# Operand addresses modulo 256 bytes in a hybrid decoder layer: rows of x and of the convolution blocks, with k and v in 272 and 256 columns

## The chip, the cores and the metric

The kernel runs on one core of a Trainium2 chip. Its metric is the device time of one execution in microseconds (us); several executions give a median. One further execution was recorded by the hardware profiler, with the start and the length of every instruction and DMA; all rows below are of that one. The engines are TensorE (PE, with its weight loads as PEld), VectorE (DVE), ScalarE (ACT), GpSimd (POOL) and SyncE (SP), which issues DMAs here.

## What is computed

One layer over L = 528 tokens: 16 learned meta tokens ahead of 512 of x, width 2048. An RMS norm and one input projection give q, k, v (8 heads of 128) and b, c, u (1024 channels each):

```python
p = n @ w_in[l]
q, k, v, gb, gc, u = jnp.split(p, ...)
o_attn = _stick_breaking_attention(rmsnorm(q), rmsnorm(k), v)
o_conv = gb * _causal_dwconv(gc * u, conv_w[l])       # three taps: t-2, t-1, t
h = h + concat(rmsnorm(o_attn), rmsnorm(o_conv)) @ w_out[l]
h = h + (silu(n2 @ w_gate[l]) * (n2 @ w_up[l])) @ w_down[l]
return h[:, N_META:]
```

q and b are needed for the 512 tokens of x alone. k and v are needed for all 528, and c and u from two tokens before the first of x on.

## The kernel before, in words

Activations lie with channels on the 128 partitions and tokens along the free axis, in fp32. An fp32 product is made of three fp32r matmuls: each operand is split into a rounded part (hi) and the rest (lo), and weights hi x hi, hi x lo and lo x hi are summed in PSUM. So a k tile of 128 channels takes three matmuls per part of the columns (lines 280, 282 and 284 in `product_steps`; 742, 743 and 744 in `block_product`; 842 to 844 in `wide_product`). A bank of PSUM holds 512 columns.

**x.** `split_x` (line 347) makes for each of 16 k tiles two tiles nh and nl of 528 columns, 2112 B a partition, which lie one behind the other in the pool npool. They are the moving operands of all input projections.

**Attention** (to about 340 us). `head` (line 480) runs k, q and v of each of 8 heads as plain products over 16 k tiles. k and v take their 528 columns in two parts of H = 264, one in each bank; q takes 512 columns from column META = 16 on. `qk_norm`, and `attend` with its `sums` and `mix`, are queued with `after(n, ...)`, which runs them n k tiles later in the middle of the next products, so ACT and DVE work beside PE. `form_blocks` (line 414) runs eight times in this stage: it loads x again, split at column C0 = 8 into two halves of CH = 260 columns, forms four sums of quadrants on DVE, splits them into hi and lo, and stores them into the DRAM tensor fc (a run of 8 x 260 columns for each partition, block and part).

**Convolution columns, plain** (340 to 416 us). Two channel tiles j = 0, 1: c and u as plain products of two parts of CH = 260 columns from C0 (line 683), b with 512 (line 688). `conv_taps` multiplies c and u, and r2 (the squared token scale), and applies the three taps; `conv_out` multiplies by b and splits the result. After b of j = 0 the attention's pools are closed and six loads on POOL's queue bring three of the four blocks from fc into the tile blk (line 701). After b of j = 1 sixteen loads (line 708) overwrite the second halves of the first eight nh and nl with the fourth block.

**Convolution columns, block products** (416 to 598 us). The other six channel tiles go two at a time, three pair products for each two (c and u for each of two tiles, and b for both): `pair_product` (line 746) computes a 2 x 2 block product with seven instead of eight block multiplications of 24 matmuls, so 168 matmuls for a pair product. Of the seven moving blocks, three come from blk (of_blk) and four from nh and nl (parts_of). A pair product writes y, z and x in banks of its own, one after the other.

**The rest** (from 598 us): `wide_product` by w_out, 512 columns; then the gated network, 22 pair products over blocks of 256 columns held in `slots` (line 851), which puts 4 elements ahead of a block and 60 behind it; then w_down in the same way.

Order of the queues: all weight loads are on SP's queue (line 172, `load_at`), each issued when its buffer comes free; loads and stores of activations are on POOL's, except those of `load_x`, `form_blocks` and a few at the end, which are on SP's. DMAs of one queue are served in the order of their issue.

Of the kernel before, what the change touches and what calls it, by code (L numbers as in the profile page):

```python
# [33 lines left out]
def hybrid_layer(ctx: ExitStack, tc: tile.TileContext, xT, w_in, w_out, w_gu, w_down, vecs, out):  # L34
# [22 lines left out]
    pp = open_pool("pp", 2, space=PSUM)  # L57
    sm = open_pool("sm", 4, space=PSUM)

    n_tmp = [0]  # L60
# [260 lines left out]

    H = L // 2
    n_hl = []
    accs = [pool.tile([P, L], F32, name=f"acc_x{i}") for i, pool in enumerate((rpool, atmp))]
# [5 lines left out]
    def x_scale():  # L330
        ve.tensor_tensor(acc, acc, accs[1], ALU.add)
        for a in (0, H):
            ps = small(f"ssx{a}")
            pe.matmul(ps[:, :H], ones, acc[:, a : a + H], start=True, stop=True)
            ve.tensor_scalar(ms[:, a : a + H], ps[:, :H], 1.0 / D, EPS, ALU.mult, ALU.add)
# [11 lines left out]
    def split_x(k):  # L347
        nh = npool.tile([P, L], F32R, tag=f"nh{k}", name=f"nh{k}")
        nl = npool.tile([P, L], F32R, tag=f"nl{k}", name=f"nl{k}")
        g = g_mix[:, k : k + 1]  # L350
        sc.activation(nh, xts[k], AF.Copy, scale=g)
        ve.scalar_tensor_tensor(nl, xts[k], g, nh.bitcast(F32), ALU.mult, ALU.subtract)
        n_hl.append((nh, nl))

    def square_x(k):
        if k < 2:
            sc.activation(accs[k], xts[k], AF.Square)
        else:
            s = t512(L, "r", 3)
            sc.activation(s, xts[k], AF.Square)  # L360
            ve.tensor_tensor(accs[k % 2], accs[k % 2], s, ALU.add)

    pk0 = pp.tile([P, 2, 512], F32, tag="pp", name="pk0")
    pq0 = pp.tile([P, 2, 512], F32, tag="pp", name="pq0")
    steps = [
        product_steps([(pk0[:, 0, :H], 0, H), (pk0[:, 1, :H], H, L)], n_hl, KT),
        product_steps([(pq0[:, 0, :], META, L)], n_hl, KT),
# [42 lines left out]
    od = {}  # L410
    C0, CH = 8, (L - 8) // 2
    fc = dram.tile([P, 4, 2, 8, CH], F32R, name="fc")

    def form_blocks(k):
# [3 lines left out]
        for i, kk in ((0, k), (2, k + 8)):  # L418
            nc.sync.dma_start(x4[:, i : i + 2], two(xT[kk][:, C0:]))
        for i, kk in ((0, k), (2, k + 8)):  # L420
# [25 lines left out]
    def qk_norm(ps, g, cols, dst, parts_of, name):  # L446
# [8 lines left out]
        cuts = [(0, cols)] if cols == SEQ else [(0, H), (H, L)]  # L455
        raw_v, s_v = (raw, s) if cols == SEQ else (two(raw), two(s))
        sc.activation(s_v, ps, AF.Square)
        sc.activation(raw_v, ps, AF.Copy, scale=g)
        split(sh, sl, s)
# [20 lines left out]
    def head(h):  # L480

        if h:
            pk = pp.tile([P, 2, 512], F32, tag="pp", name=f"pk{h}")
            product([(pk[:, 0, :H], 0, H), (pk[:, 1, :H], H, L)], n_hl)
# [5 lines left out]
        after(8 if h else 11, qk_norm(halves(pk, H), g_k, L, kn[:, :L], (kh, kl, 384), f"k{h}"))  # L490
# [12 lines left out]
        product([(pv[:, 0, :H], 0, H), (pv[:, 1, :H], H, L)], n_hl)  # L503
        vt = t512(L, "e", 2)
        ve.tensor_tensor(two(vt[:, :L]), halves(pv, H), two(r), ALU.mult)
        after(6 if h else 11, lambda: attend(h, kn, kh, kl, qn, qh, ql, vt))
# [146 lines left out]
    def conv_taps(j, c1, c2, y):  # L653

        ve.tensor_tensor(c1, c1, two(r2[:, C0:]), ALU.mult)
        ve.tensor_tensor(c1, c2, c1, ALU.mult)
        cu = c1.rearrange("p a b -> p (a b)")
        o = META - 2 - C0
        sc.activation(y, cu[:, o : o + SEQ], AF.Copy, scale=cw[:, 3 * j : 3 * j + 1])
        for t in (1, 2):  # L660
            ve.scalar_tensor_tensor(
                y, cu[:, o + t : o + t + SEQ], cw[:, 3 * j + t : 3 * j + t + 1], y, ALU.mult, ALU.add
            )
# [12 lines left out]
    for j in range(CONV_FIRST):  # L676
# [4 lines left out]
        for c in (c1, c2):  # L681
            p = pp.tile([P, 2, 512], F32, tag="pp", name="pcu")
            product([(p[:, 0, :CH], C0, C0 + CH), (p[:, 1, :CH], C0 + CH, L)], n_hl)
            sc.copy(two(c), halves(p, CH))
# [6 lines left out]
        if j == 0:  # L691
# [14 lines left out]
    for k in range(8):  # L706
        for part in range(2):
            gp.dma_start(n_hl[k][part][:, C0 + CH :], fc[:, 1, part, k])

    def parts_of(kk, a):  # L710
        return lambda part, k: n_hl[kk + k][part][:, a : a + CH]

    def of_blk(i):
        return lambda part, k: blk[:, i, part, k]

    conv_acts = [
        parts_of(0, C0), of_blk(2), of_blk(0), of_blk(1), parts_of(0, C0 + CH), parts_of(8, C0), parts_of(8, C0 + CH)
    ]
# [67 lines left out]

    def pair(acts):
        c1, c2 = halves_of("e"), halves_of("e2")
        x = pair_product(acts, two(c1), two(c2), sides)
# [3 lines left out]
    for j in range(CONV_FIRST, HEADS, 2):  # L793
        ys = []
        for m in range(2):
            c1, c2 = pair(conv_acts)
# [16 lines left out]
        for m in range(2):  # L813
            s = t512(SEQ, "e", 2)[:, :SEQ] if j == HEADS - 2 else cpool.tile([P, SEQ], F32, tag="s", name=f"sq{j}_{m}")
            with tc.high_priority(1 << 20) if j == HEADS - 2 else ExitStack():
                conv_out(j + m, gbs[m][:, META - C0 :], ys[m], slots[m][:, 0], slots[m][:, 1], s, ve)
    oc = [oc_end[:, 2], oc_end[:, 3], *(oc_mid[:, i] for i in range(HEADS - 2 - CONV_FIRST)), oc_end[:, 0], oc_end[:, 1]]
# [40 lines left out]
    def slot(pool, dt, n, tag, name, **kw):  # L858
        return slots(pool, dt, 1, n, name, tag=tag, **kw)[0]

    def pad(pool, n):
        pool.tile([P, n // 4], F32, name=f"pad_{pool.name}")

# [370 lines left out]
```

## Time and profile before

| what | value |
|---|---|
| median of 3 runs | 2044.49 us (2041.42 to 2046.47) |
| the profiled execution's own time | 2048.55 us |
| its span, first to last instruction | 2046.8 us |
| PE, DVE, ACT, POOL busy | 2032.0, 1718.8, 1051.1, 381.2 us |
| mean granted clock of TensorE | 0.998 of full speed |

The profile's page gives busy times of each engine, the chain of work that ended last, and the costliest groups of instructions. A group's mean duration is from the start to the modelled end of one instruction; matmuls are pipelined, so a matmul's duration is longer than the time from its start to the next one's start. That time, the step, is read from the start times of the timeline.

### The profile page before, as it was taken

What the parts mean: (1) busy time and instruction counts of PE and PEld (TensorE: products, weight loads), DVE (VectorE), ACT (ScalarE), POOL (GpSimd) and SP (SyncE); (2) the same over time, 40 slices, a digit from 0 to 9 for tenths busy, and PEclk for the clock granted to TensorE, in tenths of its full rate; (3) what the DMA queues carried; (4) which work ended last, traced back from release to release, by engine and by line L of the source; (5) the groups of instructions that cost most, each with busy time, mean ns of one, the idle gap of its engine ahead of it and who ended that gap; (6) DMA issues with size and microseconds to landing.
All of it is one profiled execution on the core that took longest, in us unless ns stands there. A gap on an engine that the chain in (4) does not pass through costs nothing.

```text
span 2046.8 us, 39727 instructions
## 1 busy us (share of the span) xinstructions
PE 2032.0 (99%) x16158; PEld 1969.1 (96%) x16158; DVE 1718.8 (84%) x2202; ACT 1051.1 (51%) x1517; POOL 381.2 (19%) x533
## 2 busy tenths in 40 slices
PE   9999999999999999999999999999999999999999
PEld 8999999999998888999999999999999999999999
DVE  8788878588876777998998998998998998888887
ACT  7666666344443435545555545554554544444443
POOL 0111111210015441011111111111101252223111
PEclk9999999999999999999999999999999999999999
DMA  6333344743365556566565565555555999989864
GB/s 230 100 129 116 127 138 130 254 149 104 104 211 181 184 181 205 155 174 171 150 176 150 151 175 153 154 171 158 151 174 152 274 311 314 246 237 255 231 156 89
DMA packets 161591, 361.70 MB, mean 177 GB/s; under 512 B 13568, under 2 KB 73216, under 8 KB 161408
## 3 DMA queue, kind: packets, MB, share of 16 engines
q1 hardware_dynamic: 79200, 227.94, 34.8%
q0 software_dynamic: 82208, 131.23, 24.4%
q8 instruction: 127, 2.08, 0.4%
q14 instruction: 56, 0.46, 0.1%
HBM read 278.50 MB, written 80.61 MB: 175 GB/s over the span
## 4 chain that ended last, share of the span: by engine, by line
PE 92%; DVE 3%; ACT 2%; DMA 2%; issue 2%; POOL 1%; SPq 0%; DVEq 0%; ACTq 0%; POOLq 0%
PE x L742 13%; PE x L744 13%; PE x L743 13%; PE z L742 6%; PE z L743 6%; PE z L744 6%; PE y L743 3%; PE y L742 3%; PE y L744 3%; PE po L843 2%; PE po L842 2%; PE po L844 2%; PE pv L280 2%; PE pv L284 1%; PE pv L282 1%
## 5 line engine op out<-in xcount | busy, mean ns | idle before, releaser
L188 ACT CAST s_buf<-w_buf 128x1024 fp32r<-128x1024 f32 (+2 forms) x665 | 660.5, 993 | 772.6 <-PE x L743 348.7
L189 DVE TENSOR_TENSOR s_buf<-w_buf,s_buf 128x1024 fp32r<-128x1024 f32 (+2 forms) x665 | 767.8, 1155 | 173.9 <-ACT s_buf L188 173.4
L743 PE MATMUL x<-f,s_buf 128*128 128x256 f32 x1408 | 388.5, 276 | 4.2 <-DMA f<-fx 4.2
L742 PE MATMUL x<-f,s_buf 128*128 128x256 f32 x1408 | 388.5, 276 | 0.5 <-ACT sides L772 0.5
L744 PE MATMUL x<-f,s_buf 128*128 128x256 f32 x1408 | 388.4, 276 | 0.0
L201 DVE TENSOR_TENSOR w_buf<-w_buf 128x1024 f32<-128x1024 f32 (+1 forms) x243 | 277.6, 1142 | 14.2 <-DMA w_buf<-w_in 9.9
L743 PEld LDWEIGHTS x<-f,s_buf 128*128 128x128 f32 x1408 | 265.4, 188 | 4.4 <-DMA f<-fx 4.4
L742 PEld LDWEIGHTS x<-f,s_buf 128*128 128x128 f32 x1408 | 265.3, 188 | 1.2 <-ACT sides L772 0.9
L744 PEld LDWEIGHTS x<-f,s_buf 128*128 128x128 f32 x1408 | 265.4, 188 | 0.0
L1036 POOL DMA_DIRECT2D fd<-s x147 | 104.0, 926 | 713.0 <-DVE s L295 691.8
L742 PE MATMUL z<-f,s_buf 128*128 128x256 f32 x704 | 193.6, 275 | 0.0
L743 PE MATMUL z<-f,s_buf 128*128 128x256 f32 x704 | 193.6, 275 | 0.0
L744 PE MATMUL z<-f,s_buf 128*128 128x256 f32 x704 | 193.6, 275 | 0.0
L744 PE MATMUL x<-ring,s_buf 128*128 128x256 f32 x608 | 167.3, 275 | 0.9 <-DVE s_buf L189 0.9
L742 PE MATMUL x<-ring,s_buf 128*128 128x256 f32 x608 | 167.2, 275 | 0.0
L743 PE MATMUL x<-ring,s_buf 128*128 128x256 f32 x608 | 167.2, 275 | 0.0
L744 PEld LDWEIGHTS z<-f,s_buf 128*128 128x128 f32 x704 | 132.1, 188 | 0.0
L743 PEld LDWEIGHTS z<-f,s_buf 128*128 128x128 f32 x704 | 132.1, 188 | 0.0
L742 PEld LDWEIGHTS z<-f,s_buf 128*128 128x128 f32 x704 | 132.1, 188 | 0.0
L1106 POOL DMA_DIRECT2D out_T<-d x62 | 60.3, 1002 | 300.4 <-DVE d L1114 240.7
L744 PEld LDWEIGHTS x<-ring,s_buf 128*128 128x128 f32 x608 | 114.1, 188 | 1.1 <-DVE s_buf L189 1.1
L743 PEld LDWEIGHTS x<-ring,s_buf 128*128 128x128 f32 x608 | 114.1, 188 | 0.0
(378 smaller groups left out, 5259.4 us busy)
## 6 DMA issues: line engine op xcount, KB each, us to landing
w_buf<-w_gu SPq DMA_DIRECT2D x176, 512.0 KB, 3.4
w_buf<-w_in SPq DMA_DIRECT2D x92, 512.0 KB, 3.4
fd<-s POOLq DMA_DIRECT2D x147, 256.0 KB, 5.2
w_buf<-w_down SPq DMA_DIRECT2D x96, 384.0 KB, 4.9
ring<-fd POOLq DMA_DIRECT2D x42, 768.0 KB, 9.1
w_buf<-w_out SPq DMA_DIRECT2D x32, 512.0 KB, 3.6
out_T<-d POOLq DMA_DIRECT2D x62, 256.0 KB, 5.6
fc<-st SPq DMA_DIRECT2D x8, 1040.0 KB, 6.2
```

What stands on the lines that cost most here:

```text
L188: sc.copy(hi, src)
L189: in_turn(ve.tensor_tensor(lo, src, hi.bitcast(F32), ALU.subtract), turn)
L201: in_turn(ve.tensor_tensor(sums[name], a, b, ALU.add), turn)
L280: pe.matmul(ps, wh, ah[:, a:b], start=k == 0, stop=False)
L742: pe.matmul(p, hi[:, kk], act(0, k), start=start and j == k == 0, stop=False, skip_group_check=skip)
L743: pe.matmul(p, hi[:, kk], act(1, k), start=False, stop=False, skip_group_check=skip)
L744: pe.matmul(p, lo[:, kk], act(0, k), start=False, stop=k == n - 1, skip_group_check=skip)
L842: pe.matmul(ps, hi[:, kk], ah, start=k == order[0], stop=False)
L843: pe.matmul(ps, hi[:, kk], al, start=False, stop=False)
L844: pe.matmul(ps, lo[:, kk], ah, start=False, stop=k == order[-1])
L1036: gp.dma_start(fd[c][s][:, :, k], t[:, :, i])
L1106: gp.dma_start(two(out[j]), c, accum_op=ALU.add)
```

## The change

- Rows of x: for each k tile one tile of 2 x 576 columns in place of nh and nl; hi and lo are 2304 B apart (9 x 256), and column 0 lies 12 columns into a row, and 530 columns from there on are used.
- H becomes META + 256 = 272: k and v are computed in parts of 272 and 256 columns, which lie side by side across two banks (`row_of`), so that readers see one run of 528.
- C0 becomes META - 2 = 14; the second half starts at C1 = C0 + 256, CH becomes 258, so the halves share two columns. The tile blk has 288 columns for each block, k tile and part, and starts 2 columns in; it is read from fc in runs of 258 columns.
- b of the block products uses the last 256 of the 258 columns.
- `conv_taps` works on two halves of 256; `conv_out`'s square goes into b's own buffer in place of a tile of its own.
- The DMA descriptors' scratch in each partition goes from its default size to 8192 B.

```diff
+    def pad(pool, n):
+        pool.tile([P, n // 4], F32, name=f"pad_{pool.name}")
...
-    H = L // 2
-    n_hl = []
+    H, ROW = META + T2, 2304 // 4
+    n_hl, n_rows = [], []
...
     def split_x(k):
-        nh = npool.tile([P, L], F32R, tag=f"nh{k}", name=f"nh{k}")
-        nl = npool.tile([P, L], F32R, tag=f"nl{k}", name=f"nl{k}")
+        n = npool.tile([P, 2 * ROW], F32R, tag=f"n{k}", name=f"n{k}")
+        n_row = n.rearrange("p (a t) -> p a t", a=2)[:, :, 12 : 14 + L]
+        nh, nl = (n_row[:, i, :L] for i in range(2))
...
+    def row_of(ps):
+        flat = ps.rearrange("p a b -> p (a b)")
+        return flat[:, 512 - H : 512 - H + L], [(flat[:, 512 - H : 512], 0, H), (flat[:, 512 : 512 + L - H], H, L)]
...
-        product_steps([(pk0[:, 0, :H], 0, H), (pk0[:, 1, :H], H, L)], n_hl, KT),
+        product_steps(row_of(pk0)[1], n_hl, KT),
...
-    C0, CH = 8, (L - 8) // 2
+    C0 = META - 2
+    C1, CH = C0 + T2, L - C0 - T2
...
         for i, kk in ((0, k), (2, k + 8)):
-            nc.sync.dma_start(x4[:, i : i + 2], two(xT[kk][:, C0:]))
+            for m, c in enumerate((C0, C1)):
+                nc.sync.dma_start(x4[:, i + m], xT[kk][:, c : c + CH])
...
-        ve.tensor_tensor(c1, c1, two(r2[:, C0:]), ALU.mult)
+        for m, c in enumerate((C0, C1)):
+            ve.tensor_tensor(c1[:, m], c1[:, m], r2[:, c : c + CH], ALU.mult)
         ve.tensor_tensor(c1, c2, c1, ALU.mult)
...
-            product([(p[:, 0, :CH], C0, C0 + CH), (p[:, 1, :CH], C0 + CH, L)], n_hl)
+            product([(p[:, 0, :CH], C0, C0 + CH), (p[:, 1, :CH], C1, L)], n_hl)
...
-            blk = blk_pool.tile([P, 3, 2, 8, CH], F32R, name="blk")
+            blk = blk_pool.tile([P, 8 + 48 * 288], F32R, name="blk")
+            blk = blk[:, 2 : 2 + 48 * 288].rearrange("p (i k a t) -> p i k a t", i=3, k=8, a=2)
+            pad(blk_pool, 128)
...
-                    gp.dma_start(blk[:, i, part], fc[:, n, part], max_dma_last_dim=4160)
+                    gp.dma_start(blk[:, i, :, part, :CH], fc[:, n, part])
...
-            gp.dma_start(n_hl[k][part][:, C0 + CH :], fc[:, 1, part, k])
+            gp.dma_start(n_rows[k][:, part, C0 + CH :], fc[:, 1, part, k])
...
+    def last_of(act):
+        return lambda part, k: act(part, k)[:, CH - T2 :]
...
-        gbs = pair(conv_acts)
+        gbs = pair([last_of(act) for act in conv_acts], T2)
...
-            s = t512(SEQ, "e", 2)[:, :SEQ] if j == HEADS - 2 else cpool.tile([P, SEQ], F32, tag="s", name=f"sq{j}_{m}")
+            s = t512(SEQ, "e", 2)[:, :SEQ] if j == HEADS - 2 else gbs[m]
...
-    nc = bacc.Bacc("TRN2", target_bir_lowering=False, num_devices=1)
+    nc = bacc.Bacc("TRN2", target_bir_lowering=False, num_devices=1, dynamic_dma_scratch_size=8192)
```

## Rows read from the trace of the kernel before

**Rows 1.** The page: the span, PE's busy time, the chain by engine.
```profile
span 2046.8 us, 39727 instructions
...
PE 2032.0 (99%) x16158; PEld 1969.1 (96%) x16158; DVE 1718.8 (84%) x2202; ACT 1051.1 (51%) x1517; POOL 381.2 (19%) x533
...
PE 92%; DVE 3%; ACT 2%; DMA 2%; issue 2%; POOL 1%; SPq 0%; DVEq 0%; ACTq 0%; POOLq 0%
```

**Rows 2.** Busy time by stage: attention, plain convolution columns, block products.
```profile
core 0: us, PE busy (x) PEld busy (x) DVE busy (x) ACT busy (x) POOL busy (x), PEclk, DMA share, GB/s
0.00:340.00 340.00, 337.58 (x2268) 312.88 (x2269) 278.13 (x465) 225.43 (x374) 50.78 (x114) 1.00 0.41 137
340.00:416.00 76.00, 75.62 (x523) 70.40 (x522) 46.25 (x67) 35.37 (x54) 20.35 (x39) 1.00 0.72 233
416.00:598.00 182.00, 181.23 (x1510) 180.60 (x1509) 151.25 (x166) 86.69 (x116) 13.92 (x13) 1.00 0.36 120
```

**Rows 3.** PE's waits, longest first: us in total, times, longest.
```profile
PE x L743 <- DMA f<-fx: 4.2, 1, 4.2
PE warm L85 <- DVE one L81: 1.1, 1, 1.1
```

**Rows 4.** Groups of PE matmuls by form: xcount, busy us, mean ns, idle.
```profile
L742 PE MATMUL x<-nh,s_buf 128*128 128x260 f32 x216 | 61.0, 283 | 0.5 <-ACT sides_c L772 0.5
L280 PE MATMUL pk<-nh,s_buf 128*128 128x264 f32 x256 | 53.4, 290 | 0.5 <-ACT nh L351 0.5
```

**Rows 5.** PE's timeline: start us, duration us, what; first and last of counted stretches.
```profile
283.18 0.40 PE L280 MATMUL pv<-nh,s_buf 128*128 128x264 f32 x2
...
289.69 0.39 PE L465 MATMUL ss_q<-sh_q,ones_r 128*128 128x512 f32 x1
...
303.35 0.35 PE L527 MATMUL z<-qh,kh 128*128 128x400 f32 x1
...
303.90 0.29 PE L527 MATMUL z<-qh,kh 128*128 128x272 f32 x1
...
388.96 0.40 PE L280 MATMUL pcu<-nh,s_buf 128*128 128x260 f32 x2
...
404.83 0.39 PE L280 MATMUL pb<-nh,s_buf 128*128 128x512 f32 x1
...
415.87 0.28 PE L742 MATMUL y<-nh,s_buf 128*128 128x260 f32 x1
...
500.25 0.28 PE L742 MATMUL z<-blk,s_buf 128*128 128x260 f32 x1
...
520.37 0.28 PE L742 MATMUL z<-blk,s_buf 128*128 128x260 f32 x1
...
643.91 0.39 PE L842 MATMUL po<-oa,s_buf 128*128 128x512 f32 x1
...
654.79 0.39 PE L842 MATMUL po<-oa,s_buf 128*128 128x512 f32 x1
...
1015.55 0.28 PE L742 MATMUL z<-f,s_buf 128*128 128x256 f32 x1
...
1034.59 0.28 PE L742 MATMUL z<-f,s_buf 128*128 128x256 f32 x1
```

**Rows 6.** Timelines (PE, POOL, DVE), DMA issues (KB, us to landing), one tile's transfers.
```profile
430.26 0.28 PE L742 MATMUL x<-nh,s_buf 128*128 128x260 f32 x1
...
381.80 4.33 POOL L701 DMA_DIRECT2D blk<-fc  x6 [0.30 <-POOL acc_a L314]
...
424.53 0.43 DVE L783 TENSOR_TENSOR tmp<-y,sides_c 128x260 f32<-128x260 f32 x1
...
fc<-st SPq DMA_DIRECT2D x8, 1040.0 KB, 6.2
...
DMA to landing us min/median/max: 5.6/12.8/20.4
...
L428 SPq DMA_DIRECT2D fc<-st x8: 524/525/601, 96.4 to 365.6; - x8
```

More of the change, by code (lines that the diff above doesn't have):

```diff
@@ L332, in x_scale @@
         for a in (0, H):
-            ps = small(f"ssx{a}")
-            pe.matmul(ps[:, :H], ones, acc[:, a : a + H], start=True, stop=True)
-            ve.tensor_scalar(ms[:, a : a + H], ps[:, :H], 1.0 / D, EPS, ALU.mult, ALU.add)
+            b = L if a else H
+            ps = small(f"ssx{a}")[:, : b - a]
+            pe.matmul(ps, ones, acc[:, a:b], start=True, stop=True)
+            ve.tensor_scalar(ms[:, a:b], ps, 1.0 / D, EPS, ALU.mult, ALU.add)
         rsqrt(r, ms, L)
@@ L353, in split_x @@
         n_hl.append((nh, nl))
+        n_rows.append(n_row)
     def square_x(k):
@@ L455, in qk_norm @@
         cuts = [(0, cols)] if cols == SEQ else [(0, H), (H, L)]
-        raw_v, s_v = (raw, s) if cols == SEQ else (two(raw), two(s))
-        sc.activation(s_v, ps, AF.Square)
-        sc.activation(raw_v, ps, AF.Copy, scale=g)
+        sc.activation(s, ps, AF.Square)
+        sc.activation(raw, ps, AF.Copy, scale=g)
         split(sh, sl, s)
@@ L483, in head @@
             pk = pp.tile([P, 2, 512], F32, tag="pp", name=f"pk{h}")
-            product([(pk[:, 0, :H], 0, H), (pk[:, 1, :H], H, L)], n_hl)
+            product(row_of(pk)[1], n_hl)
         else:
@@ L489, in head @@
         kl = apool.tile([P, 384], F32R, tag="kl", name=f"kl{h}")
-        after(8 if h else 11, qk_norm(halves(pk, H), g_k, L, kn[:, :L], (kh, kl, 384), f"k{h}"))
+        after(8 if h else 11, qk_norm(row_of(pk)[0], g_k, L, kn[:, :L], (kh, kl, 384), f"k{h}"))
         if h:
@@ L502, in head @@
         pv = pp.tile([P, 2, 512], F32, tag="pp", name=f"pv{h}")
-        product([(pv[:, 0, :H], 0, H), (pv[:, 1, :H], H, L)], n_hl)
+        pv_row, parts = row_of(pv)
+        product(parts, n_hl)
         vt = t512(L, "e", 2)
-        ve.tensor_tensor(two(vt[:, :L]), halves(pv, H), two(r), ALU.mult)
+        ve.tensor_tensor(vt[:, :L], pv_row, r, ALU.mult)
         after(6 if h else 11, lambda: attend(h, kn, kh, kl, qn, qh, ql, vt))
@@ L653, in conv_taps @@
     def conv_taps(j, c1, c2, y):
-        ve.tensor_tensor(c1, c1, two(r2[:, C0:]), ALU.mult)
+        for m, c in enumerate((C0, C1)):
+            ve.tensor_tensor(c1[:, m], c1[:, m], r2[:, c : c + CH], ALU.mult)
         ve.tensor_tensor(c1, c2, c1, ALU.mult)
-        cu = c1.rearrange("p a b -> p (a b)")
-        o = META - 2 - C0
-        sc.activation(y, cu[:, o : o + SEQ], AF.Copy, scale=cw[:, 3 * j : 3 * j + 1])
+        y = two(y)
+        sc.activation(y, c1[:, :, :T2], AF.Copy, scale=cw[:, 3 * j : 3 * j + 1])
         for t in (1, 2):
             ve.scalar_tensor_tensor(
-                y, cu[:, o + t : o + t + SEQ], cw[:, 3 * j + t : 3 * j + t + 1], y, ALU.mult, ALU.add
+                y, c1[:, :, t : t + T2], cw[:, 3 * j + t : 3 * j + t + 1], y, ALU.mult, ALU.add
             )
@@ L707, in hybrid_layer @@
         for part in range(2):
-            gp.dma_start(n_hl[k][part][:, C0 + CH :], fc[:, 1, part, k])
+            gp.dma_start(n_rows[k][:, part, C0 + CH :], fc[:, 1, part, k])
     def parts_of(kk, a):
-        return lambda part, k: n_hl[kk + k][part][:, a : a + CH]
+        return lambda part, k: n_rows[kk + k][:, part, a : a + CH]
     def of_blk(i):
-        return lambda part, k: blk[:, i, part, k]
+        return lambda part, k: blk[:, i, k, part, :CH]
+    def last_of(act):
+        return lambda part, k: act(part, k)[:, CH - T2 :]
     conv_acts = [
-        parts_of(0, C0), of_blk(2), of_blk(0), of_blk(1), parts_of(0, C0 + CH), parts_of(8, C0), parts_of(8, C0 + CH)
+        parts_of(0, C0), of_blk(2), of_blk(0), of_blk(1), parts_of(0, C0 + CH), parts_of(8, C0), parts_of(8, C1)
     ]
@@ L785, in pair_product, with pair @@
         return x
-    def pair(acts):
-        c1, c2 = halves_of("e"), halves_of("e2")
+    def pair(acts, n):
+        c1, c2 = (halves_of(t)[:, : 2 * n] for t in ("e", "e2"))
         x = pair_product(acts, two(c1), two(c2), sides)
@@ L795, in hybrid_layer @@
         for m in range(2):
-            c1, c2 = pair(conv_acts)
+            c1, c2 = pair(conv_acts, CH)
             ys.append(t512(SEQ, "v", 2)[:, :SEQ])
             conv_taps(j + m, two(c1), two(c2), ys[m])
-        gbs = pair(conv_acts)
+        gbs = pair([last_of(act) for act in conv_acts], T2)
         if j < HEADS - 2:
@@ L813, in hybrid_layer @@
         for m in range(2):
-            s = t512(SEQ, "e", 2)[:, :SEQ] if j == HEADS - 2 else cpool.tile([P, SEQ], F32, tag="s", name=f"sq{j}_{m}")
+            s = t512(SEQ, "e", 2)[:, :SEQ] if j == HEADS - 2 else gbs[m]
             with tc.high_priority(1 << 20) if j == HEADS - 2 else ExitStack():
-                conv_out(j + m, gbs[m][:, META - C0 :], ys[m], slots[m][:, 0], slots[m][:, 1], s, ve)
+                conv_out(j + m, gbs[m], ys[m], slots[m][:, 0], slots[m][:, 1], s, ve)
     oc = [oc_end[:, 2], oc_end[:, 3], *(oc_mid[:, i] for i in range(HEADS - 2 - CONV_FIRST)), oc_end[:, 0], oc_end[:, 1]]
@@ L859, in slot @@
         return slots(pool, dt, 1, n, name, tag=tag, **kw)[0]
-    def pad(pool, n):
-        pool.tile([P, n // 4], F32, name=f"pad_{pool.name}")
     acts = {}
```

## Prediction

> **What bounds the kernel now.** I read the page first: TensorE (PE) is busy in 2032.0 of 2046.8 us and 92% of the chain that ended last is PE [rows 1]. Then the table by stage: in the three stages that this change touches (attention to 340 us, two convolution columns by plain products to 416, six by block products to 598) PE is busy all but a few us, VectorE (DVE) at most 83% [rows 2]. Then PE's waits: the longest of the run is 4.2 us, for a load in the gated network, and the next 1.1 [rows 3]. So nothing ends late on PE in these stages; their length is the number of matmuls times the step from one start to the next. The durations, which overlap (283 and 290 ns in [rows 4]), don't show that step, the timeline's start times do.
>
> The steps, each from two starts and the matmuls between them, out of [rows 5]: k and v, 264 columns, 54 matmuls in 6.51 us, 120.6 ns; c and u by plain products, 260 columns, 132 in 15.87 us, 120.2 ns; b, 512 columns, 48 in 11.04 us, 230.0 ns; block products, 260 columns, 168 in 20.12 us, 119.8 ns; the gated network, 256 columns, 168 in 19.04 us, 113.3 ns; w_out, 512 columns, 48 in 10.88 us, 226.7 ns. The last two agree on 0.4427 ns a column with nothing added (113.3 is half of 226.7). At that rate 264 columns would take 116.9, 260 115.1 and 512 226.7. So every product out of x or blk pays 3.3 to 5.1 ns a matmul more than its columns, whatever its width.
>
> What sets these apart is in the code. nh and nl are tiles of 528 x 4 = 2112 B = 8 x 256 + 64, so from tile to tile the start moves by 64 B modulo 256; each k of blk moves by 1040 B, that is 16. In the gated network and w_out every moving operand starts at one remainder and has whole multiples of 256 B. b has such a length too, but moving remainders, and pays 3.3 ns: the remainder alone costs something. The other half, one remainder but an odd length, has one row: three steps of 400 columns over q tiles of 2048 B take 0.55 us, 183.3 ns against 177.1 at the straight rate, so 6 ns stay [rows 5]; they are three steps between others, at 10 ns resolution.
>
> **The change part by part.** It removes no matmul; counts are from [rows 4] and the loops.
> - q and b of the plain products: 384 + 96 matmuls of 512 columns get hi and lo at one remainder (112 B into a row), as w_out has. 480 x 3.3 ns = 1.6 us. Not less than nothing, since the form is that of w_out.
> - b of the block products: 3 of 9 pair products, 504 matmuls, go from 260 to 256 columns. 288 of them read rows of x, as the gated network reads its blocks: 288 x (119.8 - 113.3) = 1.9 us. The 216 on blk have hi and lo 1152 B apart, 128 modulo 256. Between 4 columns alone (1.8 ns) and all (6.5) I take the middle, as they share width but not remainder with the gated network: 0.9 us.
> - c and u: 1008 block and 384 plain matmuls go to 258 columns, one remainder on x rows. At the straight rate 114.2 ns. Columns alone give 0.9 ns each, everything 5.6 (block) and 6.0 (plain). The gated network's long steady stream speaks for the upper end, the 400-column steps for the lower; I take the middle: 1008 x 3.2 + 384 x 3.5 = 4.6 us.
> - k and v: 1536 matmuls of 264 become pairs of 272 and 256, the same columns; starts alternate between 48 and 112 B. Between 0 and 3.7 ns, the middle for the same reason: 1536 x 1.85 = 2.8 us.
> Together 11.8 us; with the upper ends 18.5, with the lower 5.1.
>
> What it adds: 16 more loads of x in form_blocks, on SP's queue ahead of the weight loads; an SP issue takes about 0.5 us [rows 6], two at a time, and no wait of PE for a weight load stands among its long ones [rows 3]. If that cover were gone, 16 x 0.5 = 8 us at most. conv_taps multiplies by r2 in two instructions, 8 more on DVE; a whole one of 260 columns takes 0.43 us [rows 6], so under 3.4 us, on an engine with idle time in all three stages. The square of y goes into gbs, which the next pair product but one overwrites, 20 us later. ScalarE and DVE read k and v as one run of 528 columns over two banks: same elements. The scratch of 8 KB could make POOL's loads wait for each other: between nothing and the doubling of PE's one long wait, 4.2 us; I take nothing, since POOL is busy 27% of a stage at most [rows 2]. A faster PE leaves the attention's chain of ACT and DVE less slack: each of its 24 sums is put six k tiles behind what it needs (36 matmuls, 4.3 us), and that lead shrinks by 1.85 in 120.6, 66 ns, so up to 1.6 us where all are at their limit already; I take off 1 us. That leaves 10.8 us.
>
> Against the profiled execution, 2048.55 us (its span and 1.75 around it), this is 2037.8; the median of the runs is 4.06 lower, so 2033.7, **2034**.
>
> The Trainium skill ("TensorE: Matmul & The Clock Gate", section "Back-to-back issue gap") gives a warm matmul N/2.4 + 2.5 ns, with no place for an address. By it 264 columns took 112.5 ns and 512 took 215.8, in b and w_out alike; no row here agrees, as 512 columns are read at 226.7 and at 230.0.
>
> **The rivals.**
> 1. Address is all that counts (upper ends): every changed product runs at 0.4427 ns a column. For it: two widths in two stages at exactly one rate. Against: the 400-column steps. 18.5 - 1 = 17.5 us, **2027**.
> 2. Width is all that counts, the change doesn't do what it says: the 3 to 5 ns come from something else in these stages (denser traffic of DMA and ACT, say). Then only columns go: 1392 x 2 + 504 x 4 = 4800 x 0.4427 ns = 2.1 us, less the 1 us: **2043**. For it: stages and addresses change together. Against: b and w_out, one width at two steps; and the block products, with the lowest DMA share of the three stages, 0.36 [rows 2], pay 4.7 ns, no less than the others. The page's rule named above, that the step follows the column count alone, is this rival's.
> 3. The other side, slower: blk comes late. Its six loads are read in runs of 8320 B now; then each k is a run of 1032 B. They are issued at 381.80, land in 5.6 to 20.4 us, and the first block that reads the halves loaded behind them on the same queue (nl, nh of line 708) starts at 430.26 [rows 6]. The nearest row with such runs is fc<-st, 1040 KB in 6.2 us: six of these and the 2.08 MB of nl and nh are 8 x 6.2 = 49.6 us, where PE, 1.2 us faster in between, leaves 47.2: 2.4 us of stall. It decides from (47.2 + 10.8)/8 = 7.3 us for 1040 KB on; at 9 us, with weight loads beside them, it is 72 - 47 = 25 us of stall against a gain of 11: 14 us slower, **2058**. Against: the loads overlap, the six together were down within 4.33 + 20.4 = 25 us.
>
> **How the numbers follow.** About 0.3%, 6.1 us, is what a measurement of this kernel can tell from no change: faster means below 2038.4. The forecast, some gain on every product, has 0.48, and about a tenth of that lies in the "same" band; rival 1 has 0.26; rival 2, all of it "same", 0.18; rival 3 0.08, of which 0.02 is a stall that just eats the gain. Faster 0.43 + 0.26 = 0.69; same 0.05 + 0.18 + 0.02 = 0.25; slower 0.06. The range runs from just below rival 1, for the runs' own spread of 2.5 us, to rival 2: 2024 to 2043; rival 3's late case and half of what lies about the ends is left out.
>
> **What would show it.** Right: b's 48 steps at 226.7 ns in plain products; the b pair products near 113.3 on x; c and u between 114.2 and 119; a k and v pair between 234 and 241 ns; everything from w_out on unchanged in length. Wrong: 230 ns for b still (rival 2); 114.2 for c and u (rival 1); an idle stretch of PE ended by a DMA of blk, nl or nh near 420 to 430 us (rival 3); waits on ACT or DVE in the attention over a few us, which would say that the gain there is given back.

## The result and the profile after

The change makes the kernel slower. Its median is 2051.91 us (8 runs, 2049.92 to 2056.51); the kernel before, run beside it, has 2043.38 (8 runs). The ratio is 1.0043, 95% interval 1.0034 to 1.0052; the medians lie 8.5 us apart. The prediction, 2034 with a range of 2024 to 2043 and 0.06 for slower, has the wrong sign. Executions of one kernel differ by some 7 us, and in the longer ones the mean granted clock of TensorE is 0.998 or 0.999 of full speed; the trace of the kernel before is of such a one (2048.55 us, 0.998) and that of the changed kernel is not, so the two are compared by stage and not by their spans.

The page of the changed kernel, against [rows 1] and the store in [rows 6]: the span, busy times, the chain by engine, two groups of the section on DMAs (KB, us to landing).

```profile
span 2050.9 us, 39794 instructions
...
PE 2032.6 (99%) x16158; PEld 1964.3 (96%) x16158; DVE 1720.7 (84%) x2210; ACT 1049.8 (51%) x1517; POOL 382.8 (19%) x533
...
PE 88%; DVE 4%; DMA 2%; ACT 2%; issue 2%; POOL 1%; SPq 0%; DVEq 0%; ACTq 0%; POOLq 0%
...
fc<-st SPq DMA_DIRECT2D x8, 1032.0 KB, 7.9
...
x<-xT SPq DMA_DIRECT2D x32, 129.0 KB, 6.5
```

PE is as busy as before (2032.6 against 2032.0), and 4% of the chain has gone from PE to others. The store into fc moves 0.8% less and takes 7.9 us instead of 6.2. The table by stage is cut at the first pcu (the PSUM tile of c and u in the plain stage, so its first matmul ends the attention), the first block product and the first w_out matmul:

```profile
0.00:348.26 348.26, 340.05 (x2265) 310.39 (x2266) 277.87 (x465) 225.32 (x374) 50.47 (x114) 1.00 0.42 133
348.26:427.02 78.76, 76.57 (x523) 70.57 (x522) 45.60 (x69) 35.16 (x53) 21.31 (x39) 1.00 0.88 222
427.02:608.73 181.71, 181.52 (x1514) 181.31 (x1513) 153.66 (x173) 86.80 (x116) 16.04 (x14) 1.00 0.38 121
```

In [rows 2] the same borders lie near 340, 416 and 598. The loss is in the first two stages: in the attention PE is idle for 8.2 us where [rows 2] have 2.4, and the plain columns take 78.8 us where they took 76.1 (339.76 to 415.87). The block products come out 0.9 us shorter (before, 415.87 to 598.47), but not by their steps: before, PE waits there twice for ScalarE, which costs some 0.5 us each time, and in the changed kernel it does not:

```profile
PE x L742 <- ACT sides_c L772: 0.5, 2, 0.3
```

From w_out on the changed kernel is 6.2 us shorter (1442.2 against 1448.3); that is the wait for f<-fx and what follows it, told with the scratch below. PE's waits, longest first, against [rows 3]:

```profile
PE ss_k L477 <- ACT sh_k L297: 2.9, 3, 1.0
PE c L601 <- DVE spl L298: 2.2, 8, 0.6
PE c L600 <- ACT sph L297: 1.2, 2, 1.0
...
PE ss_k L478 <- DVE sl_k L298: 1.1, 3, 0.4
...
PE x L761 <- DMA f<-fx: 0.9, 1, 0.9
```

New are the waits for ScalarE's and DVE's splits in the attention (ss_k, c). The wait for f<-fx, 4.2 us before, is 0.9. What makes ScalarE late stands in the group of its scaling of x in form_blocks. First the kernel before (xcount, busy, mean ns, idle before it and what ended it), then the changed one, and ScalarE's timeline in one head of the changed kernel:

```profile
L421 ACT ACTIVATE x<-x,vec 128x520 f32<-128x520 f32 x16 | 11.5, 730 | 2.6 <-DMA x<-xT 2.6
```

```profile
L434 ACT ACTIVATE x<-x,vec 128x516 f32<-128x516 f32 x16 | 11.5, 726 | 17.2 <-DMA x<-xT 17.2
```

```profile
138.58 1.79 ACT L569 ACTIVATE lw<-lw,one 128x432 f32<-128x432 f32 x3
143.90 0.73 ACT L434 ACTIVATE x<-x,vec 128x516 f32<-128x516 f32 x1 [3.53 <-DMA x<-xT]
144.53 0.54 ACT L297 CAST sph<-sp 128x432 fp32r<-128x432 f32 x1
```

ScalarE stands for 3.53 us before an activation whose data have not landed, and the attention's splits (sph here, sh_k after it) stand behind it in its order. On SP's queue the four loads of x stand right behind the store:

```profile
133.99 0.52 SPq L441 DMA_DIRECT2D fc<-st  x1
134.57 3.90 SPq L432 DMA_DIRECT2D x<-xT  x4
```

Then PE waits for the splits, in the same head:

```profile
151.28 0.39 PE L477 MATMUL ss_k<-sh_k,ones_r 128*128 128x272 f32 x1 [0.96 <-ACT sh_k L297]
152.02 0.39 PE L478 MATMUL ss_k<-sl_k,ones_r 128*128 128x272 f32 x1 [0.35 <-DVE sl_k L298]
...
159.09 0.50 PE L601 MATMUL c<-spl,carry 128*128 128x512 f32 x1 [0.21 <-DVE spl L298]
```

The steps, from start to start, in PE's timeline of the changed kernel, against [rows 5]:

```profile
289.14 0.40 PE L283 MATMUL pv<-n,s_buf 128*128 128x272 f32 x2
...
295.62 0.40 PE L477 MATMUL ss_q<-sh_q,ones_r 128*128 128x512 f32 x1
...
400.10 0.40 PE L283 MATMUL pcu<-n,s_buf 128*128 128x258 f32 x2
...
415.94 0.39 PE L283 MATMUL pb<-n,s_buf 128*128 128x512 f32 x1
...
427.02 0.28 PE L760 MATMUL y<-n,s_buf 128*128 128x258 f32 x1
...
462.31 0.29 PE L760 MATMUL y<-n,s_buf 128*128 128x258 f32 x1
...
465.27 0.29 PE L760 MATMUL x<-n,s_buf 128*128 128x258 f32 x1
...
468.23 0.28 PE L760 MATMUL x<-n,s_buf 128*128 128x256 f32 x1
...
485.17 0.28 PE L760 MATMUL x<-n,s_buf 128*128 128x256 f32 x1
...
487.89 0.28 PE L760 MATMUL x<-n,s_buf 128*128 128x258 f32 x1
...
508.26 0.29 PE L760 MATMUL x<-n,s_buf 128*128 128x258 f32 x1
```

k and v: 54 matmuls in 6.48 us, 120.0 ns (120.6 before). c and u, plain: 132 in 15.84, 120.0 (120.2). b, 512 columns: 48 in 11.08, 230.8 (230.0). A block of c or u on rows of x: 24 in 2.96, 123.3, **slower** than 119.8 although two columns shorter; a whole pair product of c and u, with its blocks from blk, 168 in 20.37, 121.3 (119.8). b's pair product: 168 in 19.66, 117.0 (119.8), and its last block 24 in 2.72, 113.3. These are single stretches. Over all matmuls of a kind, without the steps that hold a wait, the mean step in ns is:

| matmuls | before | changed |
|---|---|---|
| q; b in the plain stage (512 columns) | 230.8; 230.5 | 230.7; 230.3 |
| k and v | 120.8 | 120.6 |
| c and u, plain stage | 120.1 | 120.2 |
| c and u, blocks on rows of x; on blk | 119.6; 119.8 | 122.3; 120.0 |
| b, blocks on rows of x; on blk | 119.6; 119.8 | 116.4; 117.8 |

So one remainder modulo 256 gives the straight rate to one form of all, 256 columns at 240.

### The profile page after: what moved, and what is told of

Read it like the earlier page. It is cut to its first block, busy times and chain, and to the rows that moved or that the text cites. A ratio compares the mean times of both kernels' runs of the same rounds, so it can differ in the third digit from the quotient of the medians.

```text
span 2050.9 us, 39794 instructions
## 1 busy us (share of the span) xinstructions
PE 2032.6 (99%) x16158; PEld 1964.3 (96%) x16158; DVE 1720.7 (84%) x2210; ACT 1049.8 (51%) x1517; POOL 382.8 (19%) x533
## 4 chain that ended last, share of the span: by engine, by line
PE 88%; DVE 4%; DMA 2%; ACT 2%; issue 2%; POOL 1%; SPq 0%; DVEq 0%; ACTq 0%; POOLq 0%
PE x L760 13%; PE x L762 13%; PE x L761 13%; PE z L762 6%; PE z L760 6%; PE z L761 6%; PE y L761 3%; PE y L760 3%; PE y L762 3%; PE po L862 2%; PE po L860 2%; PE po L861 2%; PE pv L283 1%; PE pv L287 1%; PE pv L285 1%
```

## The experiments

The first three take the loads of x for the cause: the change splits each of them in two.

**Two loads again.**

```diff
-            for m, c in enumerate((C0, C1)):
-                nc.sync.dma_start(x4[:, i + m], xT[kk][:, c : c + CH])
+            row = xT[kk][:, C0 : C0 + CH]
+            nc.sync.dma_start(x4[:, i : i + 2], bass.AP(row.tensor, row.offset, [row.ap[0], [T2, 2], row.ap[1]]))
```

> The changed kernel, but form_blocks fetches each k tile's two overlapping halves of x in one DMA again: 16 loads of 258 KB in place of 32 of 129 KB, still in runs of 1032 B. Theory A (the four loads on SP's queue land too late, ScalarE stands before its x<-x activations, and what is behind them on ScalarE makes PE wait): ScalarE's idle time ended by the DMA of x falls from 17.2 us to under 5, the first pcu starts near 341 to 343 us instead of 348.3, and the median falls by 7 to 10 us, to 2042 to 2045. Theory B (the shorter runs of 1032 B in place of 2080 make them late, however many DMAs carry them): the idle time stays over 12 us and the median stays within 2 us of 2051.9. Theory C (the time went to k and v in 272 and 256 columns over two banks): no change either, but the idle time falls.

**The kernel before with four loads.**

```diff
-            nc.sync.dma_start(x4[:, i : i + 2], two(xT[kk][:, C0:]))
+            for m in range(2):
+                nc.sync.dma_start(x4[:, i + m], xT[kk][:, C0 + m * CH : C0 + (m + 1) * CH])
```

> The kernel before, with the one load of each k tile in form_blocks split into two of 130 KB, nothing else changed: 32 loads on SP's queue in place of 16. Theory A: it loses most of what the change lost, the median rises by 8 to 11 us to 2051 to 2054, with ScalarE idle 12 to 18 us in front of its x<-x activations (2.6 now). Theory B: it rises too, since the runs are 1040 B then; A and B are told apart by the run above. Theory C: within 2 us of 2043.4.

**form_blocks later in the head.**

```diff
-            after(6, lambda h=h: form_blocks(h - 2))
+            after(11, lambda h=h: form_blocks(h - 2))
```

> The changed kernel, with form_blocks queued 11 instead of 6 k tiles into a head from head 2 on, so its activations on ScalarE stand some 3.6 us later among the other work; the loads are issued as before, as soon as their buffer is free. Theory A: the loads have landed when ScalarE comes to them, its idle time before them goes under 4 us, and 6 to 10 us come back: 2042 to 2046. Theory D (the loads' traffic itself delays weight loads or stores, not ScalarE's place in its order): the median stays within 2 us of 2051.9.

All runs of the kernel stand in this table: median, ratio to before with its interval, the store's median time, ScalarE's idle time that the DMA of x ended, and the start of the first pcu (us). Before: 6.2, 2.6 and 339.76; changed: 7.9, 17.2 and 348.26.

| run | median | ratio | store | idle | first pcu |
|---|---|---|---|---|---|
| two loads again | 2050.71 | 1.0036 (1.0024 to 1.0049) | 7.6 | 12.8 | 346.01 |
| before, four loads | 2044.30 | 1.0002 (0.9993 to 1.0011) | 6.1 | 3.0 | 338.58 |
| form_blocks later | 2051.59 | 1.0044 (1.0031 to 1.0056) | 7.7 | 12.7 | 346.78 |
| x in aligned runs | 2050.61 | 1.0034 (1.0021 to 1.0047) | 8.0 | 13.2 | 348.00 |
| x, fc and blk in 260 columns | 2040.76 | 0.9985 (0.9976 to 0.9993) | 6.1 | 1.2 | 338.62 |
| before, halves of 258 | 2054.33 | 1.0045 (1.0032 to 1.0058) | 7.9 | 10.9 | 345.21 |
| c and u in 260 columns at 224 | 2040.56 | 0.9981 (0.9972 to 0.9989) | 6.3 | 3.9 | 338.14 |
| and q, b in two halves of 256 | 2040.67 | 0.9979 (0.9971 to 0.9988) | 6.4 | 4.2 | 340.08 |
| before, scratch of 8 KB | 2041.65 | 0.9986 (0.9978 to 0.9995) | 6.1 | 2.4 | 338.76 |
| store 1032 B, aligned starts | 2044.68 | 1.0005 (0.9995 to 1.0014) | 7.1 | 7.9 | 343.83 |
| store 1040 B alone | 2042.93 | 1.0000 (0.9989 to 1.0011) | 6.1 | 2.2 | 337.95 |

Theory A fell: four loads in the kernel before cost nothing, and two in the changed one bring the ratio from 1.0043 to 1.0036 alone, which is within the intervals. The idle time stayed at 12.8, which spoke for B, the short runs; but B also had the kernel before slower with four loads of 1040 B, and that missed. Queueing form_blocks later did not move its activations: the first of one head starts at 143.05 us, 14.2 after the head's first matmul of k, in the changed kernel at 143.90, 14.8 after; so that run tells nothing of ScalarE's place in its order. Theory C is out by the trace: k's and v's steps are not longer.

**Which runs.** The loads of x in aligned runs of 1040 B, then the store and blk's loads with them, and the kernel before with runs of 1032 B in the store alone of form_blocks' two transfers:

```diff
-        x4 = stage.tile([P, 4, CH], F32, tag="x4", name=f"x4_{k}")
+        xw = stage.tile([P, 4, CH + 2], F32, tag="x4", name=f"x4_{k}")
+        x4 = xw[:, :, 2:]
...
-                nc.sync.dma_start(x4[:, i + m], xT[kk][:, c : c + CH])
+                nc.sync.dma_start(xw[:, i + m], xT[kk][:, c - 2 : c + CH])
```

> The changed kernel, with the 32 loads of x in form_blocks begun two columns earlier: 260 columns (1040 B) from bytes that are multiples of 16, in place of 258 (1032 B) from bytes at 8 modulo 16, in x as well as in SBUF; the store into fc stays as it is, in runs of 1032 B. Theory H (a load whose runs start at 8 modulo 16 takes longer, so x lands too late for ScalarE): ScalarE's idle time ended by the DMA of x falls from 17.2 us to under 6, the first pcu starts at 340 to 342 us, the median is 2042 to 2045. Theory S (the store fc<-st in runs of 1032 B, 1.7 us slower and ahead of the loads on SP's queue, is what makes them late): the idle time stays over 9 us and the median over 2048. Theory T (that idle time is not what PE loses): the idle time falls and the first pcu still starts past 345 us.

```diff
-    fc = dram.tile([P, 4, 2, 8, CH], F32R, name="fc")
+    fc = dram.tile([P, 4, 2, 8, CH + 2], F32R, name="fc")
...
-                    gp.dma_start(blk[:, i, :, part, :CH], fc[:, n, part])
+                    gp.dma_start(blk[:, i, :, part, : CH + 2], fc[:, n, part])
```

> The run above, and fc, its store and the loads into blk in 260 columns too, so that these runs are 1040 B from multiples of 16 B; every matmul still reads what it reads in the changed kernel. Theories H and S: the store is back at 6.0 to 6.4 us, the idle time before the x<-x activations under 4 us, the first pcu at 339 to 341 us, the median 2041 to 2044. Theory T: the median stays over 2048.

```diff
-    C0, CH = 8, (L - 8) // 2
+    C0, CH = 12, (L - 12) // 2
```

> The kernel before with C0 = 12 and so halves of 258 columns: x is still loaded in one run of 2064 B from a multiple of 16 B, the store into fc goes out in runs of 1032 B, and the matmuls of c, u and b have 258 columns at the old pitch of 2112 B. Theory S: ScalarE is idle over 9 us before its x<-x activations and the attention ends 5 us later, near 345 us, 2047 to 2052. Theory H: the idle time stays under 5 us, the attention ends as before, near 340 us. On the steps: if 258 columns take 119 to 120 ns at any remainder, the block products take no less than with 260.

Theory S holds and H fell. With x's runs alone made whole the store stays at 8.0 us and x as late as in the other runs; with the store's too (and blk's loads) everything is back. That the ratio then lies below 1 is no more than the smaller scratch gives alone (0.9986, below). The kernel before, given a store in runs of 1032 B, loses as much as the change did; its median, 2054.33 from four executions, lies above the range expected, 2047 to 2052. Its block products, with 258 columns at the old pitch, are no shorter than with 260 (182.9 us against 182.6), as expected. Its two rows, ScalarE's group and the store:

```profile
L421 ACT ACTIVATE x<-x,vec 128x516 f32<-128x516 f32 x16 | 11.4, 726 | 12.2 <-DMA x<-xT 10.9 <-DVE lb L558 1.3
...
fc<-st SPq DMA_DIRECT2D x8, 1032.0 KB, 7.9
```

**The store alone, its length and its starts.** In the first run rows lie 260 columns apart and 258 of each are moved; in the second the whole rows are.

```diff
-        nc.sync.dma_start(fc[:, :, :, k].bitcast(F32), st.bitcast(F32))
+        nc.sync.dma_start(fc[:, :, :, k, :CH].bitcast(F32), st[:, :, :, :CH].bitcast(F32))
```

> The changed kernel with only the store into fc altered: its rows in SBUF and in fc lie 260 columns (1040 B) apart, so each run starts at a multiple of 16 B, but 258 columns (1032 B) of each are moved, as in the changed kernel; the loads of x stay at 1032 B from 8 modulo 16. If the start is what slows the store: 6.0 to 6.5 us for a store, the first pcu near 339 to 342 us, the median 2040 to 2044. If the length of 1032 B is: 7.5 to 8 us for a store, the first pcu past 345 us, the median over 2048.

```diff
+        xw = stage.tile([P, 4, CH + 2], F32, tag="x4", name=f"x4_{k}")
+        x4 = xw[:, :, :CH]
+        gp.memset(xw[:, :, CH:], 0.0)
...
-        split(st[:, :, 0], st[:, :, 1], x4)
+        split(st[:, :, 0], st[:, :, 1], xw)
```

> The changed kernel with only the store into fc altered: its rows lie 260 columns apart in SBUF and in fc and whole rows of 1040 B are moved, the last two columns of each being filler that nothing reads; the loads of x stay at 1032 B from 8 modulo 16, and a small memset on POOL fills x4's two columns. Theory S (the store alone): 6.0 to 6.5 us for a store, ScalarE's idle time before x<-x under 7 us, the first pcu at 339 to 342 us, the median 2040 to 2044. Rival (store and loads of x must both be in aligned runs): the first pcu past 344 us, the median over 2046.

The store alone is enough for the stages that lost: 6.1 us a store, the first pcu at 337.95. Its group of ScalarE, its store, and its stages, with the loads of x still split and still in runs of 1032 B:

```profile
L436 ACT ACTIVATE x<-x,vec 128x516 f32<-128x516 f32 x16 | 11.5, 727 | 3.5 <-DMA x<-xT 2.2 <-DVE lb L573 1.3
...
fc<-st SPq DMA_DIRECT2D x8, 1040.0 KB, 6.1
...
x<-xT SPq DMA_DIRECT2D x32, 129.0 KB, 5.0
...
0.00:337.95 337.95, 335.73 (x2266) 310.22 (x2266) 277.82 (x465) 225.37 (x374) 51.15 (x121) 1.00 0.42 138
337.95:413.97 76.02, 75.70 (x524) 70.46 (x522) 45.43 (x69) 35.19 (x53) 21.41 (x40) 1.00 0.88 231
413.97:595.67 181.70, 181.51 (x1513) 181.30 (x1512) 153.75 (x174) 86.81 (x116) 16.05 (x14) 1.00 0.37 121
```

The loads of x, unchanged, land in 5.0 us instead of 6.5. The median comes back to that of the kernel before (1.0000), not to the 0.9985 of the run with x, fc and blk in 260 columns; the intervals overlap, and whether there is a difference is open.

Both rivals on the form of the run are half right: 1032 B from multiples of 16 takes 7.1 us a store, between 6.1 and 7.9, and the first pcu lies half way too. In the changed kernel the runs lie end to end, 1032 B apart, so every second one starts at 8 modulo 16; its eight stores spread from 6.2 to 9.3 us, where the kernel before has 5.7 to 6.3. Whether the start in SBUF or the one in fc counts was not tested. The Trainium skill ("DMA: Bandwidth & Descriptors", section "How a descriptor splits into AXI transactions") counts beats of 32 B, cut at 256 B. By it 1032 and 1040 B are 33 beats each from such a boundary, and from any other multiple of 16 B equally many; the stores at 7.1 and 6.1 us differ, so that count does not tell them apart here.

**The matmul's step by itself.** Three runs leave the layer out and put streams of matmuls behind one another. Starts modulo 256 B follow from the order and the sizes of the tiles; the traces hold no addresses.

> The layer is left out: 26 streams of 96 or 192 fp32r matmuls each run one behind the other on data that waits in SBUF, with the kernel's order of hi and lo (two rows of one tile) and a weight load for each matmul. A stream differs from the next in columns, in the start modulo 256 B, in the pitch of the rows and in the place in PSUM. Theory E (a stream runs at 0.4427 ns a column only if its length is a multiple of 64 columns and all its starts have one remainder modulo 256 that is a multiple of 16): 113.3 ns for 256 columns at 0 and 240, about 120 at 232, 120 to 123 for 258 columns at any remainder, 226.7 for 512 at 0 and 240, whatever the pitch. Theory F (one remainder that is a multiple of 16 is enough, any length): 114.2 for 258, 115.1 for 260, 116.9 for 264 and 120.4 for 272 columns at 0 and 240. Theory G (the pitch of 2304 B hurts 512 columns): 230 to 231 for 512 at a pitch of 2304, 226.7 at 2048.

> The layer is left out: streams of 96 matmuls as in the run of streams before this, rows 2304 B apart, for 256, 258, 260, 264, 272 and 512 columns, each at the sixteen starts 0, 16, ... 240 modulo 256 B. Theory K (only certain pairs of length and start run straight): 256 columns at 113.3 ns at 240 and at a few starts beside it, 118 to 120 at 0 and most others; 512 columns at 226.7 at 128, where w_out's rows lie, and 231 to 233 at 0 and 240; for the lengths that are not multiples of 64 no start gives the straight rate (114.2, 115.1, 116.9), or one does that no row of the kernel uses. Theory E (any multiple of 16 does for 256 and 512) has already failed at 0.

The first gave 113.3 ns for 256 columns at 240, but 118.8 at 0 and 120.0 at 232; 120.0 and 118.6 for 258 columns at 0 and 240, **123.3 at 232**; 231.1 for 512 at 240 and 232 to 233 at 0, at either pitch. Theories E, F and G all fell. The second took all sixteen starts (mean step of the second half of each stream, from its start times):

| columns | straight rate | start modulo 256 at the straight rate | all other starts |
|---|---|---|---|
| 256 | 113.3 | 64, 240 | 116.7 to 120.0 |
| 258 | 114.2 | none | 116.7 to 122.2 |
| 260 | 115.1 | none | 118.3 to 121.7 |
| 264 | 116.9 | none | 120.0 to 123.3 |
| 272 | 120.4 | none | 123.3 to 126.7 |
| 512 | 226.7 | 112, 128 | 228.9 to 234.7 |

Its timeline, 256 columns at 48, 64 and 80 and 512 at 112, 128, 144 and 160; a stream's 96 steps reach to the next one's start:

```profile
54.34 11.60 PE L157 MATMUL s_ad<-x,w 128*128 128x256 f32 x96
65.77 11.07 PE L157 MATMUL s_ae<-x,w 128*128 128x256 f32 x96
76.68 11.60 PE L157 MATMUL s_af<-x,w 128*128 128x256 f32 x96
...
1105.07 21.93 PE L157 MATMUL s_dj<-x,w 128*128 128x512 f32 x96
1126.84 21.96 PE L157 MATMUL s_dk<-x,w 128*128 128x512 f32 x96
1148.64 22.40 PE L157 MATMUL s_dl<-x,w 128*128 128x512 f32 x96
1170.88 22.57 PE L157 MATMUL s_dm<-x,w 128*128 128x512 f32 x96
```

Theory K holds: 11.43, then 10.91 us for 96 of 256 columns; 21.77, 21.80, then 22.24 for 512. The straight values come again from run to run, the others not always: 264 columns at 0 took 120.0 ns in the first run and 123.3 in the second, 258 at 0 took 120.0 and 122.2. That is why w_out, with rows at 128, runs at 226.7 [rows 5], b at 240 does not, and the gated network's 256 columns at 240 do. Whether the start counts alone or against the weights' start:

> The layer is left out: streams of 96 matmuls as in the two runs of streams, with the weights 64 B further on (256 and 512 columns at sixteen starts) and 128 B further on (256 columns); then two halves of 256 in turn at 240 and at 64, 256 at 240 and 260 at 224 with lo 128 B from hi modulo 256 as in blk, and 256 with lo at 64 and hi at 240. Theory R (what counts is where the moving operand starts against the weights): the starts that run straight move along, from 64 and 240 to 128 and 48 for 256 columns with weights 64 B further on, from 112 and 128 to 176 and 192 for 512. Theory M (the moving operand's start alone): 64 and 240, 112 and 128 as before. Halves in turn at 240: 113.3 ns; at 240 with lo at 112: 117 to 118 as in the changed kernel's blk.

Theory R: with the weights 64 B on, the straight starts are 48 and 128 for 256 columns and 176 and 192 for 512; with 128 B on, 112 and 192. So for 256 columns the moving operand must start 112 or 192 B behind the weights modulo 256, for 512 columns 240 or 0. Rows at 48 and 64, and at 176, 192 and 208:

```profile
54.60 11.04 PE L114 MATMUL s_ad<-x,w 128*128 128x256 f32 x96
65.48 11.55 PE L114 MATMUL s_ae<-x,w 128*128 128x256 f32 x96
...
628.00 21.93 PE L114 MATMUL s_br<-x,w 128*128 128x512 f32 x96
649.76 21.96 PE L114 MATMUL s_bs<-x,w 128*128 128x512 f32 x96
671.56 22.40 PE L114 MATMUL s_bt<-x,w 128*128 128x512 f32 x96
```

Two halves of 256 in turn, both at 240, ran at 113.3; 256 at 240 with lo at 112, as in blk, at 117.8; and 256 with hi at 240 and lo at 64, each straight by itself, at 115.6.

**Built from this.** c and u in 260 columns, which puts every run of form_blocks on 1040 B, and then q and plain b in two halves:

```diff
-    C0 = META - 2
+    C0 = META - 4
...
-            y, c1[:, :, t : t + T2], cw
+            y, c1[:, :, 2 + t : 2 + t + T2], cw
```

> The changed kernel with C0 = META - 4 and so halves of 260 columns that share four: x, fc and blk move in runs of 1040 B from multiples of 16 B, and c and u read 260 columns at 224 modulo 256 where the changed kernel reads 258 at 232; b reads the same last 256 columns at 240. Theory S2 (runs of 1032 B in the store into fc are the loss) and the streams (258 columns at 232: 123.3 ns, 260 at 224: 120.0, b at 240: 113.3): the store at 6.0 to 6.4 us, the first pcu near 339 to 341 us, c and u products on rows of x 3 ns a matmul shorter than in the run with aligned runs, 432 x 3.3 ns = 1.4 us, so a median of 2038 to 2041 (2040.8 there). Rival: the gain of that run came from the shorter blocks, then 2041 to 2043.

```diff
-            product([(pq[:, 0, :], META, L)], n_hl)
+            product(halves_of_512(pq)[1], n_hl)
```

> The run above, with q and b of the plain products in two halves of 256 columns, both at 240 modulo 256, side by side across two banks, in place of 512 columns at 240: twice the matmuls there (960 for 480). The streams have 113.3 ns for 256 columns at 240 and 231.1 for 512 there. Theory K (pairs of length and start): a half takes 113.3 ns, 226.7 for two, 480 x 4.4 = 2.1 us less than the run above, 2036 to 2039. Rival (two halves in turn, or the change of bank, don't settle): 116 to 120 ns a half, 0.5 to 4 us more than the run above.

Both beat the kernel before and the changed one, by 0.2% and 0.6%. But both have the small scratch, which alone gives 0.9986 (next run), so what the columns give beyond it is not clear of the noise; the second, at 2040.67, also missed the range of theory K, 2036 to 2039. The first's block products are 1.1 us shorter than with 258 at 232 (180.56 against 181.70 from the first to w_out). In the second plain b's 96 halves take 10.93 us, 113.9 ns, 0.15 us less than 512 columns at 240; q's halves average 115.1 ns, 0.7 ns less for two than one of 512; in the attention that is given back, PE waits 1.4 us for ss_k, where the run before it has no such wait, and the first pcu is 1.9 us later.

**The scratch alone.**

```diff
-    nc = bacc.Bacc("TRN2", target_bir_lowering=False, num_devices=1)
+    nc = bacc.Bacc("TRN2", target_bir_lowering=False, num_devices=1, dynamic_dma_scratch_size=8192)
```

> The kernel before with the descriptors' scratch at 8192 B and nothing else changed. My prediction took nothing for it, between nothing and 4.2 us of loss. Theory N: nothing, within 1 us of the kernel before. Rival: it delays or hastens the loads on POOL's queue ahead of the gated network, where PE's wait for f<-fx was 4.2 us before and 0.9 us after; then the median moves by 1 to 4 us with that wait.

Its rival holds, as a gain: 0.9986, about 2.9 us, and no wait for f<-fx is left on PE. POOL's timeline ahead of the gated network, before and with 8 KB:

```profile
767.09 1.43 POOL L997 DMA_DIRECT2D fx<-st  x2 [6.72 <-DVE w L901]
774.98 2.86 POOL L980 DMA_DIRECT2D f<-fx  x4 [6.47 <-issue]
```

```profile
764.22 1.43 POOL L997 DMA_DIRECT2D fx<-st  x2 [4.66 <-DVE st L295]
773.85 2.86 POOL L980 DMA_DIRECT2D f<-fx  x4 [8.20 <-issue]
```

The stores of fx go out 4.66 instead of 6.72 us after POOL's work before them; the loads of f behind them are issued 1.1 us earlier and land in 8.7 us instead of 11.1, in the median of four. Why the size of the scratch brings this about was not found out. It is one trace of each: in the kernel before with four loads, which also has the default scratch, the loads take 9.3 us and the wait is 2.4.

That wait costs more than its length. In the kernel before the granted clock after it is 0.50, the level of 1.2 GHz, and some 25 matmuls of 256 columns take 214 ns from start to start instead of 113.3, 2.5 us more. Some 1 us behind the wait:

```profile
794.00:798.00 4.00, 4.00 (x21) 4.00 (x20) 0.00 (x0) 0.00 (x0) 0.00 (x0) 0.50 0.22 87
```

The same followed waits for f<-fx of 3.9 us (the kernel before with halves of 258) and 3.3 us (two loads again); behind waits of 2.4 us and less the traces show a granted clock of 1.00.

## Why the prediction was wrong

- **The store into fc was costed at nothing.** This is the step that turned the sign. The text took the store's row, 6.2 us [rows 6], as a price for blk's loads, and did not ask what runs of 1032 B do to the store itself. They make it 7.9 us; the loads of x, behind it on SP's queue, land late (6.5 us after their issue, 5.0 with the store mended); ScalarE stands 17.2 us before them; PE waits for what is behind. No run takes ScalarE's stand away by itself; that it is the link rests on the waits and on the table, where store, idle time and first pcu go together. Against the run with the store alone mended, the first block product starts 13.1 us later (427.02 and 413.97) in the two traces; by the medians' ratios it is 0.43%, 8.8 us. The difference between the two figures is not explained.
- **The 16 more loads of x** were bounded at 8 us on SP's queue and taken as hidden: right, the kernel before with four loads has 1.0002.
- **q and b, 1.6 us; c and u, 4.6; k and v, 2.8.** This is the second step that failed: with no loss in the store, the matmuls would still have given nothing. The step from "w_out and the gated network run straight" to "one remainder runs straight" failed: it is one remainder against the weights, another for each length, and none was found for 258 or 272 columns. Measured over all: q, b and the plain c and u unchanged; the six pair products of c and u 121.4 ns a step instead of 119.7, 1.7 us lost; k and v 1536 x 0.2 ns = 0.3 us gained. The row of 400 columns, which the text read for the lower end, was the one to follow: in a stream it takes 183.3 ns, as there.
- **b of the block products, 2.8 us**: 504 x 2.8 ns = 1.4. The part on x rows works, once a stream has settled; 117.8 for blk, with lo at 112, was within its bounds.
- **The attention's slack, 1 us**: not tested here, as PE did not get faster. The run with q in halves, whose new waits are for the splits of k, suggests that it is there.
- **The scratch, nothing**, with 4.2 us of loss as the bound: it is a gain of 2.9, on the side that the bound left out. The bound took the wait's length as its price; the stretch at 1.2 GHz behind it came on top.
- **The rivals.** blk did not come late: no wait of PE for a DMA between 420 and 430 us; its loads took 15.6 us instead of 12.8 in the median (they came in packets of 4160 B before, not of the 8320 B that the text has). The text did price a transfer in shorter runs, but at the wrong place. Its sign "waits on ACT or DVE in the attention" came up, though not because a gain was given back. Rival 2, 2043, is nearest to what the steps gave in sum, though not for its reason: the address does count, but the change hit the right pair of length and start in one form alone.

The sum by measured terms: the steps come to nothing (1.7 us lost in c and u, 1.4 gained in b, 0.3 in k and v) where 11.8 were forecast. By the first w_out matmul the changed kernel is 10.3 us behind (608.73 and 598.47), and the scratch gives back 2.9; that makes 7.4 of the 8.5 us between the medians, and the rest is open.

## What to carry to other kernels

When a size in a kernel changes, follow it into every DMA that it shapes, stores first: runs shortened from 1040 to 1032 B, end to end, cost each 1 MB store 1.8 us, and the cost came out two engines further on, through loads behind it on the queue and an engine that works in order. Before rows are moved for the matmul's sake, time one stream of that length at sixteen starts against the weights' start; a rate that two stages share does not say which of their addresses gives it. Take side effects such as a scratch size apart with a run of their own: here a gain of 2.9 us hid part of the loss, and is most of what three other runs gained.

## What was not expected of the hardware

- The step of an fp32r matmul with a weight load each depends on the moving operand's start against the weights' start modulo 256 B: 113.3 against 116.7 to 120.0 ns at 256 columns, 226.7 against 228.9 to 234.7 at 512. 258 columns from 232, 8 modulo 16, took 123.3 ns in their stream and in most blocks, more than 260 or 264 from most starts.
- 272 columns take 123.3 to 126.7 ns, and in turn with 256 at 240 the mean is 120.0: k's and v's pair of parts gains nothing over two of 264 at 120.0 to 120.6.
- A store of 1 MB from SBUF takes 6.1 us in runs of 1040 B, 7.1 in runs of 1032 B from multiples of 16 B, 7.9 with every second start at 8 modulo 16 (medians of eight); loads of x in runs of 1032 B alone do no harm.
- A smaller scratch for descriptors, 8 KB, made the kernel faster by 0.14% (0.05 to 0.22%).
- A wait of TensorE of 4.2 us for a load was followed by a granted clock of 0.50 for some 25 matmuls, at 214 instead of 113.3 ns each.
